# A decoder layer on one core: low parts of the first weights on GpSimd, convolution taps all on VectorE, and the compression's layout and banks moved

## The chip, the cores and the metric

The kernel runs on one core of a Trainium2 chip. The metric is device time in microseconds (us), as the median over runs. Engines are called as the profile calls them: PE (TensorE, matmuls), PEld (its weight loads), DVE (VectorE), ACT (ScalarE), POOL (GpSimd) and SP (SyncE, which here issues most DMAs). SBUF is the on-chip memory, PSUM the banks that PE writes its sums to. Each engine works through its own list of instructions strictly in order; semaphores hold an instruction until its inputs are there.

## The reference

One layer of a hybrid decoder with 256 positions and width 1024, all in float32:

```python
h = rms_norm(x, norm_mix_g)
x = x + hybrid_mixer(h, ...)        # convolution module and sparse attention, gated, one projection
x = x + cross_attention(rms_norm(x, norm_x_g), mem, xq_w, xkv_w, xo_w)
x = x + swiglu(rms_norm(x, norm_ffn_g), ffn_in_w, ffn_out_w)
return rms_norm(x, final_norm_g)
```

The change concerns the mixer. It multiplies `h` by one wide matrix whose column blocks are `u` (2048 columns for the convolution), `q` (16 heads of 64), `kc, vc, ks, vs, kw, vw` (four groups of 64 each), the logits of the heads' gates, and `g_conv, g_attn`. What it does with them:

```python
a, gt = split(u); v = a * sigmoid(gt)
v = causal_depthwise_conv(v, width=31) + bias         # 1024 channels, 31 taps each
conv_out = silu(layer_norm(v)) @ conv_pw_w
# compression: 15 blocks of 32 positions, step 16, for kc and vc
z = blocks + pos; k_cmp, v_cmp = silu(einsum("nlgd,lde->nge", z, w1)) @ w2
s_c = q @ k_cmp * scale + bias; p_cmp = softmax(s_c, masked)
# two more softmax branches, over selected blocks and over a window
o = g0 * o_cmp + g1 * o_selected + g2 * o_window
y = sigmoid(g_conv) * conv_out + sigmoid(g_attn) * o
```

With 256 positions all four blocks of 64 are selected and the window of 512 covers everything, so the two branches have the same scores and differ in their values only.

## The kernel before

**Products.** A float32 product is made of three fast matmuls: each operand is split into a high part and the rest. For a half chunk of weights (128 partitions x 1024) ACT copies the raw half to the high part (L174, names ending in `h`), and DVE subtracts that from the raw half (L175, names ending in `l`). PE then runs three groups of eight matmuls: high weights with high data, high weights with low data, low weights with high data. A chunk of 256 columns has two halves. Chunks are used in the order u0 to u7 (convolution), kc, vc, q0 to q3, ks, kw, vs, vw, ga0 to ga3 (`g_attn`), gc0 to gc3 (`g_conv`), then the values and keys of the cross attention and so on, up to the FFN (`f`, `fo`).

**Buffers.** The raw halves of all chunks take turns in four SBUF buffers (tag `w`, 512 KB each), the high parts in five (`whi`) and the low parts in five (`wlo`). SP issues the transfer of a raw half as soon as its buffer is free, that is when ACT's copy and the subtraction of the half four places earlier are done. So the low part of one half decides when the half four places later can start to load.

**Order.** A scheduler of the tile framework simulates the program when it is built, and writes each engine's list in the order of that simulation. A lower priority number goes first; `behind(marks)` makes an instruction come after given ones. `in_line()` keeps matmuls in program order. `convolve(...)` emits taps of the convolution with a priority 1500 later than the place where they stand: they fill time that the engine has left in the simulation.

**Convolution.** Channels come in eight blocks of 128 (`vt`), each with 31 taps over 256 positions. Before, two generators share them. `taps_v` runs 108 taps and their starts on DVE, with accumulators in two PSUM banks (tag `pt`). `taps_g` lets ACT multiply (L419, 104 products of 128x256) and POOL add pairs of blocks in SBUF (L421, 61 sums of 128x512), with every sixth product on POOL (L417). `joined` adds the parts. `yt` holds the result, `ysum` its sum over blocks for the layer norm.

**Compression.** `kvt` holds kc and vc by position. `hidden()` makes `z_ps`, 32 matmuls whose moving operand takes every 16th position, and from it `zz`. `compressed()` multiplies `zz` by the second layer, into `kc_ps` (bank `s0`) and `vc_ps` (bank `o`). `nsc` holds the scores of the compressed branch, first their bias (from `cb_ps`, L469), to which DVE adds `cs_ps` (L676).

**Attention.** Heads go in eight pairs. For a pair PE writes scores `s` (L712, L714), DVE evicts them with the bias `nb` and takes the extremes (L717, L722), ACT takes the exponentials (L732, L736), DVE scales (L744, L746), PE transposes into `pt_a`, `pt_b` (L757), ACT copies them to `ptt_a`, `ptt_b` (L760), and PE multiplies by the values into `o` (L767 to L775). For the compressed branch DVE and ACT normalise `nsc` (L814 to L826), PE transposes it into `pc_ps` (L858), ACT copies it to `pct` (L860); `vals` (L839) holds the values. The gc chunks are multiplied in between the first pairs.

**End.** Of the FFN's last part, sums of `fo` weights called `tr` (L1084) are made on DVE in `side` for a product of seven blocks with fewer multiplications; the first four of them stand early, around 483 us.

Of the kernel before, what the change touches and what calls it, by code (L numbers as in the profile page):

```python
# [97 lines left out]
def tile_hybrid_block(  # L98
# [71 lines left out]
    def split(w, shape, name):  # L170
        hi = small(f"{name}h", shape, F32R, tag="whi", bufs=5)
        lo = small(f"{name}l", shape, F32R, tag="wlo", bufs=5)
        with behind(*first.get(name, ())):
            copy = nc.scalar.activation(hi, w, AF.Copy)  # L174
            splits[name] = copy, nc.vector.tensor_tensor(out=lo, in0=w, in1=f(hi[:]), op=ALU.subtract)  # L175
# [215 lines left out]

    yt = long("yt", 6)

    def taps_v(j, ts, out):

        acc = [aux(f"yp{j + i}", [P, S], "pt", 2) for i in range(2)]
        for t in ts:
            for i in range(2):
                k = j + i
                v, w = vt[k][:, t:t + S], col(PP_DW + TAPS * k, t)  # L400
                if t == ts[0]:
                    nc.vector.tensor_scalar(out=acc[i], in0=v, scalar1=w, scalar2=col(PP_DB, k) if t == 0 else 0.0,
                                            op0=ALU.mult, op1=ALU.add)
                else:
                    nc.vector.scalar_tensor_tensor(out=out[:, i] if t == ts[-1] else acc[i], in0=v, scalar=w,  # L405
                                                   in1=acc[i], op0=ALU.mult, op1=ALU.add)
                yield

    def taps_g(j, ts):

        y = yt[:, j:j + 2]
        for t in ts:
            pr = y if t == 0 else small(f"vw{j}_{t}", [P, 2, S], tag="vw", bufs=4)
            for i in range(2):
                v, w = vt[j + i][:, t:t + S], col(PP_DW + TAPS * (j + i), t)
                if t % MIX == MIX - 1:
                    nc.gpsimd.tensor_scalar(out=pr[:, i], in0=v, scalar1=w, scalar2=0.0, op0=ALU.mult, op1=ALU.add)  # L417
                else:
                    nc.scalar.activation(pr[:, i], v, AF.Identity, scale=w, bias=col(PP_DB, j + i) if t == 0 else 0.0)  # L419
            if t > 0:  # L420
                nc.gpsimd.tensor_tensor(out=y, in0=y, in1=pr, op=ALU.add)  # L421
            yield

    def joined(j, other):
        nc.gpsimd.tensor_tensor(out=yt[:, j:j + 2], in0=yt[:, j:j + 2], in1=other, op=ALU.add)
        yield


    part01, part67 = (small(n, [P, 2, S], tag="pr", bufs=4) for n in ("part01", "part67"))
    taps = range(TAPS)  # L430
    on_v = chain(taps_v(0, taps[FIRST_G:], part01), taps_v(2, taps, yt[:, 2:4]), taps_v(6, taps[LAST_G:], part67))
    on_g = chain(taps_g(0, taps[:FIRST_G]), joined(0, part01), taps_g(6, taps[:LAST_G]), taps_g(4, taps), joined(6, part67))

    def convolve(n_v, n_g, *marks):

        here = tc.cur_priority
        tc.cur_priority = here + 1500
        with behind(*marks):
            for _ in range(n_v):
                next(on_v, None)  # L440
            for _ in range(n_g):
                next(on_g, None)
# [21 lines left out]
    nsc = small("nsc", [P, 2, HEADS, 16])  # L464
    cb_ps = aux("cb_ps", [P, 2, 16, HEADS], "s", 2)
    for qb in range(2):
        for i, ns in enumerate(CGROUPS):
# [1 line left out]
            nc.tensor.matmul(cb_ps[:, qb, n0:n1].rearrange("p n h -> p (n h)"), lhsT=cbt[:, i, qb * P:qb * P + P],  # L469
                             rhs=relt[:, RT_CB + 16 * n0:RT_CB + 16 * n1], start=True, stop=True)  # L470
# [19 lines left out]
    zz = small("zz", [P, 2, 4 * 64], tag="pr", bufs=4)  # L490
    nc.vector.memset(zz, 0.0)
    kvt = [long(f"{n}t", slot, (P, GROUPS + 1, S)) for n, slot in (("k", 11), ("v", 13))]
    for kv, name in enumerate(("kc", "vc")):
# [2 lines left out]
        nc.scalar.activation(kc[0:64, 0:GROUPS:2, :], ps[0:64], AF.Copy)
        nc.scalar.activation(kc[64:128, 0:GROUPS:2, 0:S - 1], ps[0:64, :, 1:S], AF.Copy)
        nc.scalar.activation(kc[0:64, 1:GROUPS:2, :], ps[64:128], AF.Copy)
        act = nc.scalar.activation(kc[64:128, 1:GROUPS:2, 0:S - 1], ps[64:128, :, 1:S], AF.Copy)
        nc.vector.memset(kc[:, GROUPS], 0.0)  # L500
        vec = nc.vector.tensor_copy(kc[:, GROUPS, 0:32:2], ppt[:, PP_POS + 16 * kv:PP_POS + 16 * kv + 16])
        convolve(10 - 2 * kv, 5, act, vec)
# [6 lines left out]
    def hidden():  # L509
# [3 lines left out]
        for l in range(16):  # L513
            for kv in range(2):
                nc.tensor.matmul(z_ps[HD * kv:HD * kv + HD], lhsT=w1t[:, kv, l], rhs=kvt[kv][:, :, 2 * l:2 * l + 16 * (NCMP - 1) + 1:16],
                                 start=l == 0, stop=l == 15)
# [13 lines left out]
    def compressed():  # L530

        kc_ps = aux("kc_ps", [P, GROUPS, 16], "s0", 1)
        nc.tensor.matmul(kc_ps, lhsT=ppt[:, PP_W2K:PP_W2K + P], rhs=zz[:, 0, :64].rearrange("p (g n) -> p g n", g=GROUPS),
# [880 lines left out]
```

## Time and profile before

| | us |
|---|---|
| median of 3 runs | 558.39 (558.24 to 559.12) |
| profiled execution | 558.58 |
| its span | 556.7 |
| PE busy in the span | 544.6 |
| DVE busy | 469.2 |
| ACT busy | 387.6 |
| POOL busy | 147.7, most of it between 46 and 179 us |

The span is that of the engines' instructions; 1.9 us of the execution lie around it. In rows of a timeline the first number is the start from the span's beginning, the second the duration, `x8` a run of eight like instructions, and a bracket gives the idle time ahead of the row and what ended it. The ends of matmuls are modelled and overlap, so starts are compared with starts. The granted clock of PE is 1.00 over the whole span.

### The profile page before, as it was taken

What the parts mean: (1) busy time and instruction counts of PE and PEld (TensorE: products, weight loads), DVE (VectorE), ACT (ScalarE), POOL (GpSimd) and SP (SyncE); (2) the same over time, 40 slices, a digit from 0 to 9 for tenths busy, and PEclk for the clock granted to TensorE, in tenths of its full rate; (3) what the DMA queues carried; (4) which work ended last, traced back from release to release, by engine and by line L of the source; (5) the groups of instructions that cost most, each with busy time, mean ns of one, the idle gap of its engine ahead of it and who ended that gap; (6) DMA issues with size and microseconds to landing.
All of it is one profiled execution on the core that took longest, in us unless ns stands there. A gap on an engine that the chain in (4) does not pass through costs nothing. (4 is left out here: it accounts for less than half of the span.)

```text
span 556.7 us, 10584 instructions
## 1 busy us (share of the span) xinstructions
PE 544.6 (98%) x3976; PEld 505.3 (91%) x3976; DVE 469.2 (84%) x874; ACT 387.6 (70%) x724; POOL 147.7 (27%) x121
## 2 busy tenths in 40 slices
PE   9999999989999999999999999999999999999995
PEld 8999999989999998998999999988888888788884
DVE  3889998999989998895768676577899998799896
ACT  4678769999777897779646655466666676566653
POOL 0006999999998000300003100150000000000000
PEclk9999999999999999999999999999999999999999
DMA  8949725434563554335555733444646664454632
GB/s 303 400 137 323 281 92 160 155 104 166 156 225 106 170 195 131 98 109 170 189 180 177 273 118 98 172 146 159 218 153 192 200 203 161 152 174 167 195 108 75
DMA packets 29154, 97.31 MB, mean 175 GB/s; under 512 B 3120, under 2 KB 5680, under 8 KB 28848
## 3 DMA queue, kind: packets, MB, share of 16 engines
q1 hardware_dynamic: 28384, 95.42, 51.4%
q10 hardware_dynamic: 720, 1.23, 0.6%
q8 instruction: 31, 0.51, 0.4%
q14 instruction: 19, 0.16, 0.1%
HBM read 95.39 MB, written 1.25 MB: 174 GB/s over the span
## 5 line engine op out<-in xcount | busy, mean ns | idle before, releaser
L421 POOL TENSOR_TENSOR yt<-yt,vw 128x512 f32<-128x512 f32 x61 | 102.0, 1673 | 49.8 <-DVE yp L405 46.2
L419 ACT ACTIVATE vw<-vt,ppt 128x256 f32<-128x256 f32 x104 | 45.4, 498 | 8.6 <-POOL yt L421 8.3
L1140 PE MATMUL ps_f<-g,f_0h 128*128 128x512 f32 x176 | 48.4, 397 | 1.2 <-DVE ab L1144 1.2
L1140 PE MATMUL ps_f<-g,f_1h 128*128 128x512 f32 x176 | 48.9, 397 | 0.0
L405 DVE SCALAR_TENSOR_TENSOR yp<-vt,ppt,yp 128x256 f32<-128x256 f32 x108 | 45.4, 477 | 0.2
L1140 PEld LDWEIGHTS ps_f<-g,f_1h 128*128 128x128 f32 x176 | 32.8, 188 | 7.5
L1140 PEld LDWEIGHTS ps_f<-g,f_0h 128*128 128x128 f32 x176 | 30.0, 188 | 5.4 <-DVE ab L1144 1.4
L175 DVE TENSOR_TENSOR f_1l<-f,f_1h 128x1024 fp32r<-128x1024 f32 x22 | 27.5, 1248 | 4.4 <-ACT f_1h L174 2.6
L1142 PEld LDWEIGHTS ps_f<-g,f_0l 128*128 128x128 f32 x176 | 27.0, 189 | 3.9
L174 ACT ACTIVATE f_1h<-f 128x1024 fp32r<-128x1024 f32 x22 | 23.3, 1057 | 7.3 <-PE ps_xo L239 3.7
L175 DVE TENSOR_TENSOR f_0l<-f,f_0h 128x1024 fp32r<-128x1024 f32 x22 | 26.8, 1218 | 1.7 <-ACT f_0h L174 1.7
L1142 PE MATMUL ps_f<-g,f_0l 128*128 128x256 f32 x176 | 28.2, 282 | 0.0
L1142 PE MATMUL ps_f<-g,f_1l 128*128 128x256 f32 x176 | 26.5, 281 | 0.0
L174 ACT ACTIVATE f_0h<-f 128x1024 fp32r<-128x1024 f32 x22 | 23.1, 1051 | 1.3 <-PE ps_xo L239 1.3
L732 ACT ACTIVATE p<-p,mins 128x256 f32<-128x256 f32 x32 | 15.9, 502 | 10.7 <-DVE mins L717 10.7
L1142 PEld LDWEIGHTS ps_f<-g,f_1l 128*128 128x128 f32 x176 | 23.3, 188 | 0.0
L1143 ACT ACTIVATE ab<-ps_f 128x256 f32<-128x256 f32 x44 | 16.5, 376 | 8.8 <-PE ps_f L1142 8.1
L1144 DVE TENSOR_TENSOR ab<-ps_f,ab 128x256 f32<-128x256 f32 x44 | 18.3, 419 | 4.5 <-ACT ab L1143 4.2
L283 ACT ACTIVATE uh<-sl 128x256 fp32r<-128x256 f32 x22 | 9.1, 415 | 15.8 <-DVE sl L1148 15.8
L1147 ACT ACTIVATE sl<-ab 128x256 f32<-128x256 f32 x22 | 9.2, 417 | 13.6 <-DVE ab L1145 13.5
L923 POOL COPY acc<-s_wo 128x256 f32<-128x256 f32 x1 | 0.7, 658 | 63.6 <-ACT s_wo L916 63.6
L417 POOL TENSOR_SCALAR vw<-vt,ppt 128x256 f32<-128x256 f32 x18 | 16.1, 905 | 0.5
(621 smaller groups left out, 1682.9 us busy)
## 6 DMA issues: line engine op xcount, KB each, us to landing
f<-in_wst_dram SPq DMA_DIRECT2D x44, 512.0 KB, 5.4
fo<-in_wfo_dram SPq DMA_DIRECT2D x22, 512.0 KB, 3.7
u<-in_wst_dram SPq DMA_DIRECT2D x14, 512.0 KB, 6.2
q<-in_wst_dram SPq DMA_DIRECT2D x8, 512.0 KB, 5.4
ga<-in_wst_dram SPq DMA_DIRECT2D x8, 512.0 KB, 4.4
gc<-in_wst_dram SPq DMA_DIRECT2D x8, 512.0 KB, 4.6
v<-in_wst_dram SPq DMA_DIRECT2D x8, 512.0 KB, 6.5
pw<-in_wst_dram SPq DMA_DIRECT2D x8, 512.0 KB, 4.3
```

The source lines that it names most:

```text
L174: copy = nc.scalar.activation(hi, w, AF.Copy)
L175: splits[name] = copy, nc.vector.tensor_tensor(out=lo, in0=w, in1=f(hi[:]), op=ALU.subtract)
L405: nc.vector.scalar_tensor_tensor(out=out[:, i] if t == ts[-1] else acc[i], in0=v, scalar=w, in1=acc[i], op0=ALU.mult, op1=ALU.add)
L417: nc.gpsimd.tensor_scalar(out=pr[:, i], in0=v, scalar1=w, scalar2=0.0, op0=ALU.mult, op1=ALU.add)
L419: nc.scalar.activation(pr[:, i], v, AF.Identity, scale=w, bias=col(PP_DB, j + i) if t == 0 else 0.0)
L421: nc.gpsimd.tensor_tensor(out=y, in0=y, in1=pr, op=ALU.add)
L732: exp.append(nc.scalar.activation(p1[k][:, br], p1[k][:, br], AF.Exp, scale=-1.0, bias=mins[:, hd, 1, br:br + 1], accum_out=sums[:, hd, 1, ...
L1140: nc.tensor.matmul(ps, lhsT=hs[kb // 4][0][:, kb % 4, cs], rhs=fg[:, :, kb], start=kb == 0, stop=False)
L1142: nc.tensor.matmul(ps[:, 1], lhsT=hs[kb // 4][1][:, kb % 4, cs], rhs=fg[:, 0, kb], start=False, stop=kb == NB - 1)
L1143: nc.scalar.activation(ab[:, b], ps[:, 0], AF.Copy)
L1144: nc.vector.tensor_tensor(out=ab[:, b], in0=ps[:, 1], in1=ab[:, b], op=ALU.add)
L1147: silu = nc.scalar.activation(sl, ab[:, 0], AF.Silu)
```

## The change

It has five parts.

1. `split` makes the low parts of u1 to ga1 on GpSimd (POOL) in place of DVE: 38 halves (`aside`).
2. All 248 taps run on DVE, block pair by block pair, with accumulators in the two PSUM banks `pt`. ACT's products and POOL's sums and joins are gone. POOL keeps `ysum`.
3. `kvt` is laid out by place within a block of 16, so that the moving operand of `z_ps` is contiguous. `hidden()` follows q1 as a whole (`in_line`). `compressed()` puts both products into one bank `o` and follows vs.
4. Banks: `rel_ps` goes to `s0`, `cb_ps` to `o` and into line ahead of kc, the second `cs_ps` to `o`, `gt_ps` to `s0`. Copies of q go by 64x512 in place of 64x256. The low parts of ga2_1 and ga3_1 are told to come after the sums into `nsc`.
5. The first `tr` sums at the end stand behind the marks of the last FFN part.

```diff
@@ split @@
+            eng = nc.gpsimd if name[:-2] in aside else nc.vector
-            splits[name] = copy, nc.vector.tensor_tensor(out=lo, in0=w, in1=f(hi[:]), op=ALU.subtract)
+            splits[name] = copy, eng.tensor_tensor(out=lo, in0=w, in1=f(hi[:]), op=ALU.subtract)
+    aside = CHUNKS[CHUNK_AT["u1"]:CHUNK_AT["ga2"]]
@@ convolution @@
+    def tapped(j):
         acc = [aux(f"yp{j + i}", [P, S], "pt", 2) for i in range(2)]
+        for t in range(TAPS):
             for i in range(2):
                 k = j + i
                 v, w = vt[k][:, t:t + S], col(PP_DW + TAPS * k, t)
+                if t == 0:
+                    nc.vector.tensor_scalar(out=acc[i], in0=v, scalar1=w, scalar2=col(PP_DB, k), op0=ALU.mult, op1=ALU.add)
                 else:
+                    nc.vector.scalar_tensor_tensor(out=yt[:, k] if t == TAPS - 1 else acc[i], in0=v, scalar=w, in1=acc[i],
+                                                   op0=ALU.mult, op1=ALU.add)
                 yield
-    def taps_g(j, ts):
...
+    taps = chain(*[tapped(j) for j in range(0, NB, 2)])
-        convolve((0, 4, 6, 6, 8, 8, 10, 12)[j], (0, 2, 3, 3, 4, 4, 4, 4)[j], act, vec)
+        convolve(13 * (j > 0), act, vec)
@@ tables @@
-    rel_ps = aux("rel_ps", [P, 384], "s", 2)
+    rel_ps = aux("rel_ps", [P, 384], "s0", 1)
-    cb_ps = aux("cb_ps", [P, 2, 16, HEADS], "s", 2)
+    cb_ps = aux("cb_ps", [P, 2, 16, HEADS], "o", 1)
...
+    last[:] = [mm]
@@ compression @@
-    kvt = [long(f"{n}t", slot, (P, GROUPS + 1, S)) for n, slot in (("k", 11), ("v", 13))]
+    kvt = [long(f"{n}t", slot, (P, 8, GROUPS + 1, 16)) for n, slot in (("k", 11), ("v", 13))]
...
-                nc.tensor.matmul(z_ps[HD * kv:HD * kv + HD], lhsT=w1t[:, kv, l], rhs=kvt[kv][:, :, 2 * l:2 * l + 16 * (NCMP - 1) + 1:16],
-                                 start=l == 0, stop=l == 15)
+        with in_line():
+                    mm = nc.tensor.matmul(z_ps[HD * kv:HD * kv + HD], lhsT=w1t[:, kv, l],
+                                          rhs=kvt[kv][:, l % 8, :, l // 8:l // 8 + NCMP], start=l == 0, stop=l == 15)
...
-        kc_ps = aux("kc_ps", [P, GROUPS, 16], "s0", 1)
-        vc_ps = aux("vc_ps", [P, 2, HD], "o", 1)
+        c_ps = aux("c_ps", [P, 3, HD], "o", 1)
...
-        with behind(*last):
-            if j == 0:
-                hidden()
-            elif j == 2:
-                compressed()
+        if j == 1:
+            hidden()
...
-        convolve(2 * TAPS * br, 3 + TAPS * br, act, splits[name + "_1"][1])
+        convolve(13 + NB * TAPS * br, act, splits[name + "_1"][0])
+        if not br:
+            compressed()
@@ scores of the compressed branch, gates @@
-            cs_ps = aux(f"cs_ps{qb}", [P, HEADS, 2, 16], ("s", "pt")[qb], 2)
+            cs_ps = aux(f"cs_ps{qb}", [P, HEADS, 2, 16], *(("s", 2), ("o", 1))[qb])
...
+            first[("ga2_1", "ga3_1")[qb]] = added,
-    gt_ps = aux("gt_ps", [P, 2, ng], "o", 1)
+    gt_ps = aux("gt_ps", [P, 2, ng], "s0", 1)
@@ end @@
-        for n in range(4):
-            side(tr, w, n)
+        with behind(*marks if i == SEVEN[1] else ()):
+            for n in range(4):
+                side(tr, w, n)
```

How the lists of the engines move is seen at three places. In these rows a line number is that of the kernel they are from (the change's lines are some 2 to 21 lower), and a number behind a name tells apart buffers of one name in program order.

First PE, around the compression's second layer. Before, in the middle of q3 and ks:

```order
L239 MATMUL ps_q_1586<-hl,q_1h 128x256 x3
L533 MATMUL kc_ps<-zz,ppt 128x64
L239 MATMUL ps_q_1586<-hl,q_1h 128x256 x5
L239 MATMUL ps_q_1586<-hh,q_1l 128x256 x8
L239 MATMUL ps_ks<-hh,ks_0h 128x256 x8
L239 MATMUL ps_ks<-hl,ks_0h 128x256 x2
L538 MATMUL vc_ps<-ppt,zz 128x64 x2
L239 MATMUL ps_ks<-hl,ks_0h 128x256 x6
```

With the change, between vs and vw:

```order
L239 MATMUL ps_vs<-vs_1h,hl 128x256 x8
L239 MATMUL ps_vs<-vs_1l,hh 128x256 x8
L514 MATMUL c_ps<-zz,ppt 128x64
L517 MATMUL c_ps<-ppt,zz 128x64 x2
L239 MATMUL ps_vw<-vw_0h,hh 128x256 x8
```

Both products of `zz` stand three chunks later and together.

Second DVE, where the scores of the compressed branch are summed and their softmax begins. Before:

```order
L676 TENSOR_TENSOR nsc<-cs_ps_2152,nsc 128x256 x2
L814 TENSOR_REDUCE mc<-nsc 128x32
L815 TENSOR_TENSOR nsc<-nsc,mc 128x512
L739 SCALAR_TENSOR_TENSOR sums<-sums,igd 128x8
L175 TENSOR_TENSOR gc_1l<-gc_1_2432,gc_1h 128x1024
```

With the change:

```order
L654 TENSOR_TENSOR nsc<-cs_ps_2011,nsc 128x256
L174 TENSOR_TENSOR ga_1l<-ga_1_2201,ga_1h 128x1024
L174 TENSOR_TENSOR gc_0l<-gc_0_2261,gc_0h 128x1024
L174 TENSOR_TENSOR gc_1l<-gc_1_2291,gc_1h 128x1024
L407 SCALAR_TENSOR_TENSOR yp_1718<-vt_354,ppt,yp_1718 128x256
L407 SCALAR_TENSOR_TENSOR yp_1717<-vt_354,ppt,yp_1717 128x256
L793 TENSOR_REDUCE mc<-nsc 128x32
```

Taps of the last pair of blocks (`yp_1717`, `yp_1718`) stand between the steps, and three splits ahead of `mc`. Further on, eight more taps stand between the reduction `sumc` and the last product into `nsc`; behind that product the order is as before: eight evictions of the second head pair, `vals`, and the split of gc1's first half.

Third ACT, where the first head pair's transposed weights are copied. Before:

```order
L174 ACTIVATE gc_1h<-gc_1_2730 128x1024
L860 ACTIVATE pct<-pc_ps 128x512
L760 ACTIVATE ptt_a_2465<-pt_a_2460 128x512
L760 ACTIVATE ptt_a_2472<-pt_a_2467 128x512
L760 ACTIVATE ptt_b_2479<-pt_b_2474 128x512
L732 ACTIVATE p_2_2384,sums<-p_2_2384,mins 128x256 x2
```

With the change:

```order
L172 ACTIVATE gc_0h<-gc_0_2505 128x1024
L799 ACTIVATE nsc<-nsc 128x512
L625 ACTIVATE sga<-ps_ga_2170 128x512
L172 ACTIVATE gc_1h<-gc_1_2589 128x1024
L839 ACTIVATE pct<-pc_ps 128x512
L172 ACTIVATE gc_0h<-gc_0_2660 128x1024
L739 ACTIVATE ptt_a_2324<-pt_a_2319 128x512
L739 ACTIVATE ptt_a_2331<-pt_a_2326 128x512
L739 ACTIVATE ptt_b_2338<-pt_b_2333 128x512
L711 ACTIVATE p_2_2243,sums<-p_2_2243,mins 128x256 x2
```

The copy of gc3's first half (`gc_0_2660`) now stands ahead of the three copies; before, it stood behind them and behind the exponentials of the second pair. The copy of gc2's first half (`gc_0_2505`) now stands ahead of the exponential of `nsc`; before, it stood behind it.

More of the change, by code (lines that the diff above doesn't have):

```diff
@@ L31 @@
 NCMP = 15
-MIX = 6
-FIRST_G, LAST_G = 23, 10
 WARM = 10
@@ L400, in taps_v, with convolve @@
                 v, w = vt[k][:, t:t + S], col(PP_DW + TAPS * k, t)
-                if t == ts[0]:
-                    nc.vector.tensor_scalar(out=acc[i], in0=v, scalar1=w, scalar2=col(PP_DB, k) if t == 0 else 0.0,
-                                            op0=ALU.mult, op1=ALU.add)
-                else:
-                    nc.vector.scalar_tensor_tensor(out=out[:, i] if t == ts[-1] else acc[i], in0=v, scalar=w,
-                                                   in1=acc[i], op0=ALU.mult, op1=ALU.add)
+                if t == 0:
+                    nc.vector.tensor_scalar(out=acc[i], in0=v, scalar1=w, scalar2=col(PP_DB, k), op0=ALU.mult, op1=ALU.add)
+                else:
+                    nc.vector.scalar_tensor_tensor(out=yt[:, k] if t == TAPS - 1 else acc[i], in0=v, scalar=w, in1=acc[i],
+                                                   op0=ALU.mult, op1=ALU.add)
                 yield
-    def taps_g(j, ts):
[L411 to L434, printed above, removed]
+    taps = chain(*[tapped(j) for j in range(0, NB, 2)])
+    def convolve(n, *marks):
         here = tc.cur_priority
@@ L438, in convolve @@
         with behind(*marks):
[L439 to L442, printed above, removed]
+            for _ in range(n):
+                next(taps, None)
         tc.cur_priority = here
@@ L495, in tile_hybrid_block @@
         kc = kvt[kv]
[L496 to L502, printed above, removed]
+        for g in range(2):
+            for odd in range(2):
+                at = ps[HD * g:HD * g + HD].rearrange("p b (m l o) -> p b l m o", l=8, o=2)[:, :, :, :, odd]
+                act = nc.scalar.activation(kc[HD * odd:HD * odd + HD, :, g:GROUPS:2].rearrange("p l b m -> p b l m"), at, AF.Copy)
+        nc.vector.memset(kc[:, :, GROUPS], 0.0)
+        vec = nc.vector.tensor_copy(kc[:, :, GROUPS, 0:2],
+                                    ppt[:, PP_POS + 16 * kv:PP_POS + 16 * kv + 16].rearrange("p (m l) -> p l m", m=2))
+        convolve(14, act, vec)
     kcp = small("kcp", [P, GROUPS, 2, 16], F32R)
@@ L530, in compressed @@
     def compressed():
-        kc_ps = aux("kc_ps", [P, GROUPS, 16], "s0", 1)
-        nc.tensor.matmul(kc_ps, lhsT=ppt[:, PP_W2K:PP_W2K + P], rhs=zz[:, 0, :64].rearrange("p (g n) -> p g n", g=GROUPS),
-                         start=True, stop=True)
-        part(kcp[:, :, 0], kcp[:, :, 1], kc_ps[:])
-        vc_ps = aux("vc_ps", [P, 2, HD], "o", 1)
-        for i in range(2):
-            nc.tensor.matmul(vc_ps[:, i], lhsT=zz[:, 1, i * P:i * P + P], rhs=ppt[:, PP_W2V:PP_W2V + HD],
-                             start=True, stop=True)
+        c_ps = aux("c_ps", [P, 3, HD], "o", 1)
+        kc_ps, vc_ps = c_ps[:, 0].rearrange("p (g n) -> p g n", g=GROUPS), c_ps[:, 1:3]
+        with in_line():
+            nc.tensor.matmul(kc_ps, lhsT=ppt[:, PP_W2K:PP_W2K + P], rhs=zz[:, 0, :64].rearrange("p (g n) -> p g n", g=GROUPS),
+                             start=True, stop=True)
+            for i in range(2):
+                mm = nc.tensor.matmul(vc_ps[:, i], lhsT=zz[:, 1, i * P:i * P + P], rhs=ppt[:, PP_W2V:PP_W2V + HD],
+                                      start=True, stop=True)
+        last[:] = [mm]
+        part(kcp[:, :, 0], kcp[:, :, 1], kc_ps)
         nc.scalar.activation(vcs, vc_ps, AF.Copy)
@@ L675, in compressed_scores @@
             for i in range(2):
-                nc.vector.tensor_tensor(out=nsc[:, qb], in0=cs_ps[:, :, i], in1=nsc[:, qb], op=ALU.add)
+                added = nc.vector.tensor_tensor(out=nsc[:, qb], in0=cs_ps[:, :, i], in1=nsc[:, qb], op=ALU.add)
+            first[("ga2_1", "ga3_1")[qb]] = added,
     few = compressed_scores()
```

37 lines of the change are left out of this document (17 added, 20 removed).

## The prediction

> **What bounds the kernel now.** I read the page's table of engines first, then the waits of PE, then PE's timeline at each of those waits.
>
> ```profile
> PE 544.6 (98%) x3976; PEld 505.3 (91%) x3976; DVE 469.2 (84%) x874; ACT 387.6 (70%) x724; POOL 147.7 (27%) x121
> 82.44 2.02 PE L469 MATMUL cb_ps<-tables 128*128 128x48 f32 x16 [0.85 <-DVE vt L449]
> 118.96 0.43 PE L533 MATMUL kc_ps<-zz,ppt 128*128 128x64 f32 x2 [1.11 <-DVE zz L525]
> 123.44 0.63 PE L538 MATMUL vc_ps<-ppt,zz 128*128 128x64 f32 x4 [1.28 <-DVE zz L527]
> 164.62 0.47 PE L712 MATMUL s<-kdh,qt 128*128 128x512 f32 x1 [0.40 <-DVE nsc L676]
> 485.40 1.20 PE L1140 MATMUL ps_f<-g,f_0h 128*128 128x512 f32 x4 [1.22 <-DVE ab L1144]
> ```
>
> PE is busy 98% of the span. Work taken off another engine therefore buys only what PE waits for, and behind PE's start these five rows are all that it waits for: 0.85 + 1.11 + 1.28 + 0.40 + 1.22 = 4.86 us. Every other microsecond that DVE, ACT or POOL saves is worth nothing, while a new wait of PE costs its full length.
>
> **What the change removes.** The four stalls up to 165 us have causes that the diff takes away. cb_ps moves from a bank of the scores in the middle of kc to the place right behind u7, in a bank of its own. The two products of the compression's second layer stood inside q3 and ks, right behind a DVE result; they now follow vs, two to three chunks of weights later. The cs_ps tiles no longer hold the bank that s_1 needs. At 485 us DVE stood in front of a tr sum whose fo half had not landed; that sum is now held behind the last FFN part. I count all five as gone: -3.64 us up to 165 and -1.22 behind. If one stays, its own row is its price.
>
> **The compression's keys** are written by place so that z_ps reads them contiguously.
>
> ```profile
> 99.69 0.31 PE L515 MATMUL z_ps<-vt,w1t 128*64 128x75 f32 x1
> 99.82 0.31 PE L515 MATMUL z_ps<-vt,w1t 128*64 128x75 f32 x1
> 187.22 0.44 PE L772 MATMUL o<-ptt_b,vals 128*64 128x128 f32 x4
> 187.49 0.60 PE L775 MATMUL o<-ptt_a,vals 128*64 128x256 f32 x4
> ```
>
> A strided pair starts every 0.13 us, 0.065 a record; four records of the same height with a contiguous operand take 0.27, 0.068 each. So I put the layout at 0. Were half of the 32 pairs' time to go it would be -2.1, at worst strided writes by ACT cost a few tenths off PE's path.
>
> **Low parts on POOL.** 38 halves of 128x1024 leave DVE. Before shows POOL only at 128x512 and 128x256.
>
> ```profile
> 166.48 1.29 POOL L421 TENSOR_TENSOR yt<-yt,vw 128x512 f32<-128x512 f32 x1
> 50.74 10.76 POOL L421 TENSOR_TENSOR yt<-yt,vw 128x512 f32<-128x512 f32 x6
> 297.24 0.80 POOL L925 TENSOR_TENSOR acc<-acc,s_wo 128x256 f32<-128x256 f32 x1
> 119.88 1.11 PE L239 MATMUL ps_q<-hh,q_1l 128*128 128x256 f32 x8
> 120.83 1.11 PE L239 MATMUL ps_ks<-hh,ks_0h 128*128 128x256 f32 x8
> ```
>
> From 0.80 to 1.29 is 1.9 ns an element, so 1024 take 1.29 + 512 x 1.9 = 2.27 us when POOL runs freely. The upper bound is twice the disturbed 10.76/6 = 1.79, 3.6 us. PE uses one half in three groups of 0.95, 2.85 us. I take 2.5: the disturbed sums ran beside DVE splits with two operands in SBUF, and those splits leave while the taps that stay read one operand from PSUM. So POOL keeps up: 0, with a cover of 0.35 us a half. With 3.2 it would fall 38 x 0.35 = 13 us behind, less the 3 us that five buffers give.
>
> **The taps** all go to DVE, 248 instead of 108 on it. ACT's 45 us of products disappear, and with them nothing that PE waits for. Five taps stand between 157.30 and 159.26 below: 0.39 each. 140 x 0.39 = 55 us come, 38 x 1.14 = 43 us of splits go (1.14 from 185.32 to 186.46). DVE gets some 11 us more up to 190 us. Its order carries the last 25 taps into the stage of scores and softmax, in between the steps of nsc. That is where I see the loss.
>
> ```profile
> 157.30 2.04 DVE L405 SCALAR_TENSOR_TENSOR yp<-vt,ppt,yp 128x256 f32<-128x256 f32 x5
> 159.26 0.86 DVE L405 SCALAR_TENSOR_TENSOR part<-vt,ppt,yp 128x256 f32<-128x256 f32 x2
> 162.09 0.47 PE L712 MATMUL s<-kdh,qt 128*128 128x512 f32 x1
> 170.06 0.41 DVE L717 CUSTOM_DVE_ANT_0 p<-s,nb 128x256 f32<-128x256 f32 x1
> 172.28 0.87 DVE L676 TENSOR_TENSOR nsc<-cs_ps,nsc 128x256 f32<-128x256 f32 x2
> 175.76 0.63 ACT L820 ACTIVATE nsc<-nsc 128x512 f32<-128x512 f32 x1 [0.67 <-DVE nsc L815]
> 176.30 1.05 ACT L174 ACTIVATE gc_0h<-gc 128x1024 fp32r<-128x1024 f32 x1
> 178.07 0.62 DVE L821 TENSOR_REDUCE sumc<-nsc 128x32 f32<-128x512 f32 x1
> 178.06 0.33 SPq L203 DMA_DIRECT2D gc<-in_wst_dram  x1
> 181.75 1.06 ACT L174 ACTIVATE gc_1h<-gc 128x1024 fp32r<-128x1024 f32 x1 [1.54 <-DMA gc<-in_wst_dram]
> 181.90 0.42 DVE L717 CUSTOM_DVE_ANT_0 p<-s,nb 128x256 f32<-128x256 f32 x1
> 182.72 0.60 PE L858 MATMUL pc_ps<-cpt,nsc 128*128 128x128 f32 x4
> 184.12 1.29 DVE L839 TENSOR_TENSOR vals<-vcs,cpt 128x512 f32<-128x512 f32 x2
> 184.21 1.08 ACT L760 ACTIVATE ptt_a<-pt_a 128x512 f32<-128x512 f32 x2
> 185.32 1.22 DVE L175 TENSOR_TENSOR gc_0l<-gc,gc_0h 128x1024 fp32r<-128x1024 f32 x1
> 185.64 0.53 ACT L732 ACTIVATE p<-p,mins 128x256 f32<-128x256 f32 x1
> 186.46 1.22 DVE L175 TENSOR_TENSOR gc_1l<-gc,gc_1h 128x1024 fp32r<-128x1024 f32 x1
> 186.57 1.47 SPq L203 DMA_DIRECT2D gc<-in_wst_dram  x2
> 190.69 1.06 ACT L174 ACTIVATE gc_0h<-gc 128x1024 fp32r<-128x1024 f32 x1 [0.94 <-DMA gc<-in_wst_dram]
> 191.65 0.49 ACT L732 ACTIVATE p<-p,mins 128x256 f32<-128x256 f32 x1
> ```
>
> **The new wait.** Raw halves share four buffers, so the first half of gc3 takes the buffer of gc1's first half, and its transfer starts when DVE has made that half's low part: split from 185.32, issued at 186.57, ACT copies it at 190.69, 4.1 us after the issue (the half issued at 178.06 took 3.7; I use 4.0). Before, this copy stands behind the ptt copies and the exponentials, and costs only ACT 0.94. The changed order puts it ahead of the three ptt copies, for which PE's o waits. On DVE the split is still behind the last nsc product, eight evictions and vals, and that row is now later for the taps.
>
> Step by step. PE fills the first scores at 162.09 - 3.24 = 158.85, so DVE's evictions begin near 159.5 (at 158.9 if nothing delays them, near 160.2 if the queue of taps is full). Then 2.22 for eight evictions, four taps 1.56, two sums 0.9, ga3's and gc0's splits 2 x 1.14: 166.5. That split frees the buffer of gc2's first half, whose copy now stands ahead of nsc's exponential on ACT: 4.0 to its start, 0.96, and 0.54 for the exponential, 172.0. From the reduction to the end of the last product before takes 181.90 - 178.07 = 3.83, now with eight taps, 3.12, in between: 178.95. That is the time at which PE reaches pc_ps (182.72 - 3.64 = 179.08), so nothing is lost yet. Evictions 2.22, vals 1.20, gc1's split 1.14: 183.5. Transfer 4.0, copy 0.96, three ptt copies 185.64 - 184.21 = 1.43 and 0.3 to the start on PE: 190.2. PE would be there at 187.22 - 3.64 = 183.6: a stall of 6.6 us, which leaves PE 3.0 us later than before. Both gaps that I chose can shift this by about 1 us either way.
>
> One head pair later the scaling on DVE waits for exponentials that now start behind the late ptt copies: 0 to 0.9 us, I take 0.5.
>
> **PE after a long idle.** No stall of before is longer than 1.28 us, so what 6.6 us do to the clock is not in it. Its start gives one bound.
>
> ```profile
> 1.05 4.63 PE L337 MATMUL warm<-ones 128*128 128x128 f32 x20 [1.05 <-DVE eps_t L157]
> 5.48 7.42 PE L269 MATMUL ps_k<-mem_t,k0w 128*128 128x256 f32 x32
> ```
>
> The first 20 records start every 4.43/20 = 0.22 us for 128 columns; the next take 0.23 for 256 columns of the same type. So PE ran at half pace for 4.4 us and lost 2.2, although the granted clock reads 1.00. After the stall the loss lies between 0 (the 1.28 us rows) and 2.2; I take the middle, 1.1, as 6.6 us is far from both. The Trainium skill, TensorE: Matmul & The Clock Gate, Part 1, says that an idle window of about 3.4 us drops the array to half rate and that it takes some 3.4 us of work to return. By that rule the term is an estimated 1.7 and the sum 0.6 higher; the start's rows agree in kind, with 4.4 us.
>
> **Sum**, against the profiled execution's 558.58 us (span 556.7): +3.0 - 1.22 + 0.5 + 1.1 = +3.4, 562.0. The median of the runs is 0.19 lower, so 561.8.
>
> **Rivals.** *No hold-up* (0.20, faster): gc3's half is there in time, or the evictions come early enough that PE hardly waits. Speaking for it: the chain has nine steps, each sized from a different place. Against: the buffer's release at 185.32 and the issue at 186.57 are in the trace, and only the order on ACT has to be as written. It would leave -4.86 and about 1 us of DVE's lateness at the next head pair: 554.5. *Half a hold-up* (0.12, no change): the chain 3 us shorter, a stall under 3.6 us without the clock's loss: 3.4 - 3.0 - 1.1 = -0.7, about 558. *POOL too slow* (0.10, slower): it decides from 2.85 + 3/38 = 2.93 us a half. At 3.2 it adds 10 us that PE waits for in u to ga, and the hold-up shrinks since DVE is then less behind: 565 to 570. For it: 1.79 disturbed. Against: what disturbed it leaves.
>
> **How the numbers follow.** My forecast, slower through the hold-up on ACT, has 0.58, with its own range 559.6 to 564.6 from the bounds above. What can be told from no change is 0.2%, 1.1 us. Slower has 0.58 + 0.10 = 0.68, same 0.12, faster 0.20. The range from 554.6 to 565.5 leaves out about half of the faster rival and most of the one with POOL, under 2 in 10.
>
> **What would show it.** Right: a wait of PE o on ACT ptt_b of 5 to 8 us near 183 to 191, ACT idle before gc_0h on a transfer, POOL's 128x1024 at 2.2 to 2.8 us, none of the five rows above. Wrong: no such wait, waits of PE on POOL low parts between 45 and 145 us, or the five stalls replaced by others of DVE.

## The result, and the profile after

The changed kernel takes 564.86 us (median of 4 runs, 564.24 to 565.86); the kernel before, beside it, 558.75. The ratio is 1.0106, with a 95% interval of 1.0088 to 1.0125: 1.1% slower. The forecast was 561.8 and slower. The profiled execution has a span of 563.0 us, 6.3 more than before. Executions of any kernel that ran over 1.5% longer than its fastest one, at a lower granted clock, are left out of all times below.

The engines' line of the page, then the list of PE's waits (in total, how many, the longest), both of the changed kernel:

```profile
PE 543.6 (97%) x3976; PEld 504.5 (90%) x3976; DVE 464.7 (83%) x956; ACT 343.7 (61%) x606; POOL 117.7 (21%) x78
```

```profile
PE pt_a L736 <- DVE yt L407: 8.5, 1, 8.5
PE pc_ps L837 <- DVE nsc L805: 2.5, 1, 2.5
```

Left out is the row of PE's start, 1.1 us before and after. All five waits of before are gone. In their place stand two, both on DVE, and the longer one is not the one that was forecast: PE waits at the first head pair's transposes for `yt`, the last taps of the convolution. PE's timeline there:

```profile
177.53 0.66 PE L837 MATMUL pc_ps<-cpt,nsc 128*128 128x128 f32 x4 [2.46 <-DVE nsc L805]
186.67 1.97 PE L736 MATMUL pt_a<-cpt,p 128*128 128x128 f32 x8 [8.48 <-DVE yt L407]
192.65 0.59 PE L746 MATMUL o<-pct,vals 128*128 128x256 f32 x2
```

What PE waits for is on DVE (timeline of the same stage):

```profile
170.84 0.69 DVE L800 TENSOR_REDUCE sumc<-nsc 128x32 f32<-128x512 f32 x1 [2.07 <-ACT nsc L799]
...
176.79 0.68 DVE L805 TENSOR_TENSOR nsc<-nsc,sumc 128x512 f32<-128x512 f32 x1
179.61 1.28 DVE L818 TENSOR_TENSOR vals<-vcs,cpt 128x512 f32<-128x512 f32 x2
180.82 1.22 DVE L174 TENSOR_TENSOR gc_0l<-gc,gc_0h 128x1024 fp32r<-128x1024 f32 x1
...
184.23 1.21 DVE L174 TENSOR_TENSOR gc_1l<-gc,gc_1h 128x1024 fp32r<-128x1024 f32 x1
185.36 0.87 DVE L407 SCALAR_TENSOR_TENSOR yp<-vt,ppt,yp 128x256 f32<-128x256 f32 x2
186.14 0.86 DVE L407 SCALAR_TENSOR_TENSOR yt<-vt,ppt,yp 128x256 f32<-128x256 f32 x2
```

The taps accumulate in two PSUM banks of the tag `pt`, and the two `pt_a` of a head pair take turns in the same two. The last four taps stand behind `vals` and four splits, so the first bank comes free at 186.6 and the second at 187.0, while PE was ready at 178.19.

DVE is not busy all the way there. At 168.77 it stops for 2.07 us until ACT's exponential of `nsc` is done. ACT has that exponential behind its copy of gc2's first half, and the copy waits for a transfer:

```profile
169.23 1.06 ACT L172 ACTIVATE gc_0h<-gc 128x1024 fp32r<-128x1024 f32 x1 [1.90 <-DMA gc<-in_wst_dram]
```

DVE works without a break from there to the last tap. So, as an estimate from these rows, about 2 of the 2.46 us at pc_ps, and about 2 us of the lateness of the taps, come from ACT's order at this copy. No run changes this copy alone.

PE's start at the same records, changed kernel minus before, gives the balance (us; negative is ahead):

| place (start before) | difference | what happened since the row above |
|---|---|---|
| third group of ks (124.68) | -7.39 | cb, kc and vc stalls gone, `z_ps` faster |
| gc0 (178.9) | -7.82 | products of `zz` moved here, s stall gone |
| pc_ps (182.72) | -5.19 | wait of 2.46 |
| pt_a (183.16) | +3.51 | wait of 8.48 |
| o (186.69) | +5.96 | PE at half pace |
| FFN sums (475.82) | +5.89 | nothing |
| after the tr sums (488.31) | +4.40 | ps_f stall gone |
| last product (547.70) | +5.43 | waits below what the list shows |
| end of the span | +6.3 | DVE's last rows |

The half pace is in the granted clock. These are stretches of 4 us with the busy time of PE, its weight loads, DVE, ACT and POOL (in brackets the number of instructions); the next column is the clock (1.00 in the stretch ahead of these), the last two are DMA:

```profile
178.00:182.00 4.00, 0.18 (x2) 0.00 (x0) 4.00 (x18) 0.60 (x1) 0.00 (x0) 0.61 0.11 32
182.00:186.00 4.00, 0.00 (x0) 0.00 (x0) 4.00 (x6) 0.00 (x0) 0.00 (x0) 0.50 0.75 227
186.00:190.00 4.00, 3.33 (x16) 3.33 (x17) 1.01 (x3) 2.73 (x4) 2.76 (x3) 0.50 0.71 236
190.00:194.00 4.00, 4.00 (x28) 3.52 (x29) 1.53 (x3) 4.00 (x18) 0.52 (x1) 0.68 0.31 110
```

From pt_a to o PE took 5.98 us, and 3.53 before: 2.45 lost.

The forecast hold-up stands in the same trace. The changed kernel's ACT:

```profile
186.10 1.06 ACT L172 ACTIVATE gc_0h<-gc 128x1024 fp32r<-128x1024 f32 x1 [7.29 <-DMA gc<-in_wst_dram]
187.82 0.60 ACT L739 ACTIVATE ptt_a<-pt_a 128x512 f32<-128x512 f32 x1 [0.66 <-PE pt_a L736]
```

and SP's queue, with the transfer that this copy waits for, issued behind DVE's split from 180.82:

```profile
182.10 1.48 SPq L203 DMA_DIRECT2D gc<-in_wst_dram  x2
```

ACT is idle for 7.29 us on the transfer, 4.0 us from issue to copy. But the copy ends at 187.16, and ACT gets the first pt_a only at 187.82. So the two limits lie less than a microsecond apart, and the trace alone does not say what would be left if one were gone.

The last two views answer the steps on POOL (groups, mean ns) and on `z_ps` (PE's timeline):

```profile
L174 POOL TENSOR_TENSOR u_1l<-u,u_1h 128x1024 fp32r<-128x1024 f32 x7 | 18.2, 2603 | 0.0
L174 POOL TENSOR_TENSOR q_0l<-q,q_0h 128x1024 fp32r<-128x1024 f32 x4 | 9.7, 2433 | 1.2 <-ACT q_0h L172 1.2
```

```profile
101.81 0.23 PE L493 MATMUL z_ps<-kt,w1t 128*64 128x75 f32 x1
101.88 0.23 PE L493 MATMUL z_ps<-kt,w1t 128*64 128x75 f32 x1
```

A low part takes POOL 2.4 to 2.6 us, and PE never waits for one. A pair of `z_ps` records starts every 0.065 us; before, every 0.13.

### The profile page after: what moved, and what is told of

It reads as the page before. It is cut to its first block, busy times and chain, and to the rows that moved or that the text cites. A ratio compares the mean times of both kernels' runs of the same rounds, so it can differ in the third digit from the quotient of the medians.

```text
span 563.0 us, 10472 instructions
## 1 busy us (share of the span) xinstructions
PE 543.6 (97%) x3976; PEld 504.5 (90%) x3976; DVE 464.7 (83%) x956; ACT 343.7 (61%) x606; POOL 117.7 (21%) x78
## 4 chain that ended last, share of the span: by engine, by line
PE 83%; DVE 9%; DMA 5%; ACT 1%; issue 1%; ACTq 0%; DVEq 0%; SPq 0%
PE ps_f L1120 15%; PE ps_u L239 8%; PE ps_f L1122 7%; PE ps_pw L239 4%; PE ps_q L239 4%; PE ps_xq L239 4%; PE ps_wo L239 4%; PE ps_v L239 4%; PE ps_xo L239 4%; PE ps_gc L239 3%; PE ps_k L239 3%; PE ps_ga L239 3%; DMA fo<-in_wfo_dram 3%; DVE fo_1l L174 2%; DVE tr L1063 2%; PE pt_a L736 1%
## 5 line engine op out<-in xcount | busy, mean ns | idle before, releaser
L407 DVE SCALAR_TENSOR_TENSOR yp<-vt,ppt,yp 128x256 f32<-128x256 f32 x232 | 93.7, 480 | 0.3
L174 POOL TENSOR_TENSOR u_0l<-u,u_0h 128x1024 fp32r<-128x1024 f32 x7 | 17.6, 2512 | 32.1 <-DVE kt L476 30.3
L174 POOL TENSOR_TENSOR u_1l<-u,u_1h 128x1024 fp32r<-128x1024 f32 x7 | 18.2, 2603 | 0.0
L736 PE MATMUL pt_a<-cpt,p 128*128 128x128 f32 x64 | 9.3, 292 | 8.5 <-DVE yt L407 8.5
L172 ACT ACTIVATE fo_1h<-fo 128x1024 fp32r<-128x1024 f32 x10 | 10.6, 1056 | 8.9 <-DMA fo<-in_wfo_dram 5.5
```

The costliest lines, as they stand in the source:

```text
L174: splits[name] = copy, eng.tensor_tensor(out=lo, in0=w, in1=f(hi[:]), op=ALU.subtract)
L407: nc.vector.scalar_tensor_tensor(out=yt[:, k] if t == TAPS - 1 else acc[i], in0=v, scalar=w, in1=acc[i], op0=ALU.mult, op1=ALU.add)
L736: mm = nc.tensor.transpose(ps[:, i], src, ident)
```

## The experiments

Three explanations were open. *The copy on ACT*: the forecast, gc3's first half ahead of the ptt copies. *The shared bank*: pt_a cannot start before the last tap has left it. *Too much work on DVE*: neither place is the cause, DVE has more to do between 140 and 190 us than time, and whatever comes last in its order makes PE wait.

### The copy on ACT put behind the ptt copies

```diff
         if hp == 0:
+            first["gc3_0"] = copies[-1],
```

> The change, with one edit: gc3's first half is copied by ACT behind the first pair's three ptt copies; banks and everything else as changed. Theory A (the hold-up is ACT's copy of gc3's half standing ahead of the ptt copies): the stall of 8.5 us goes, and the 2.4 us of slow PE behind it; about 554. Theory B (the transposes wait for the two PSUM banks that the last pair's taps hold until 187 us): the wait of pt_a on DVE yt stays at 8 to 8.5 us; 564 to 565.

Measured: 564.06 us (562.98 to 565.70), ratio to before 1.0089 (1.0056 to 1.0122), not to be told from the change. PE's longest wait:

```profile
PE pt_a L736 <- DVE yt L407: 8.0, 1, 8.0
```

The place of this copy is not what binds in the changed kernel. The copy of gc2's first half stays ahead of the exponential of `nsc` here, and DVE waits 2.01 us for it as before.

### The last taps without the shared banks

The last pair of blocks accumulates in `yt` itself, in SBUF.

```diff
-        acc = [aux(f"yp{j + i}", [P, S], "pt", 2) for i in range(2)]
+        acc = [yt[:, j + i] if j == 6 else aux(f"yp{j + i}", [P, S], "pt", 2) for i in range(2)]
```

> The change, with one edit: the taps of the last pair of blocks accumulate in SBUF (in yt itself) and not in the two PSUM banks. The order that the scheduler then writes also puts gc3's copy on ACT behind the ptt copies, so neither hold is left. Both theories: no wait of pt_a on yt, PE not over 3 us idle there, no slow stretch of PE; 564.9 - 8.5 - 2.4 = about 554. If a third thing holds the transposes, the time stays over 558.

Measured: 563.55 us (561.80 to 569.82, three executions), ratio 1.0105 (1.003 to 1.018); about 554 was expected. The profiled execution took 561.8. The scheduler also moved gc3's copy behind the ptt copies, so this run has neither hold. PE's waits:

```profile
PE pt_a L736 <- DVE p L725: 2.7, 1, 2.7
PE s L691 <- DVE nsc L654: 2.6, 1, 2.6
PE pc_ps L837 <- DVE nsc L805: 1.6, 1, 1.6
PE pt_b L736 <- DVE mins L701: 0.8, 1, 0.8
```

The wait for `yt` is gone, so the bank was what held pt_a. But it is not what the time was lost by alone: four waits for other rows of DVE take its place, 7.7 us in place of 11.0, and the time is not to be told from that of the change. At `o` PE is 1.36 us ahead of the kernel before, and behind the gc chunks, at `mu`, 3.07 late.

### The same, with gc3's copy forced ahead of the ptt copies

For this the splits of gc1, gc2 and gc3's first half are also written earlier in the program, with a later priority; the lines below show only the order on ACT.

```diff
+        if hp == 0:
...
+            hold.append(splits["gc3_0"][0])
...
-        copies.append(nc.scalar.activation(t, ps, AF.Copy))
+        with behind(*hold):
+            copies.append(nc.scalar.activation(t, ps, AF.Copy))
```

> As the run with the free banks, but gc3's copy is put ahead of the ptt copies on ACT as in the change. Theory A as a limit of its own: PE does its transposes early and then waits at o for ptt_b until about 189 us (186.1 + 1.06 + 1.4 + 0.3 in the changed kernel's times), a stall of 5 to 8 us; 559 to 563. Theory B alone: no such stall, about 554.

Measured: 565.72 us (565.01 to 566.78), ratio 1.0118 (1.0082 to 1.0154). PE's timeline:

```profile
192.23 0.69 PE L752 MATMUL o<-ptt_b,vals 128*64 128x128 f32 x4 [5.93 <-ACT ptt_b L740]
```

This is the forecast wait, of the forecast size (6.6 forecast, 5.93 measured). Ahead of it PE is 0.99 us ahead of the kernel before, behind it 5.01 late: 6.0 us. So the mechanism exists and costs nearly what was worked out, where pt_a does not hold PE ahead of it. In the changed kernel it does. The time is above the 559 to 563 that were expected: PE also waits 2.7 us at `s`, 1.7 at pc_ps and 0.8 at pt_b, much as in the run before.

### Parts 3 and 4 alone

The kernel before, with the layout, the moved products and the banks; taps, low parts and the tr sums as before.

```diff
-            eng = nc.gpsimd if name[:-2] in aside else nc.vector
+            eng = nc.vector
...
-    taps = chain(*[tapped(j) for j in range(0, NB, 2)])
+    on_v = chain(taps_v(0, taps[FIRST_G:], part01), taps_v(2, taps, yt[:, 2:4]), taps_v(6, taps[LAST_G:], part67))
+    on_g = chain(taps_g(0, taps[:FIRST_G]), joined(0, part01), taps_g(6, taps[:LAST_G]), taps_g(4, taps), joined(6, part67))
```

> The kernel before with only the compression's layout and place, the banks, the merged copies of q and the held splits of ga2 and ga3 (parts 3 and 4); low parts and taps as before, tr sums as before. If the 7.8 us that PE is ahead by at gc in the changed kernel come from these parts: 558.5 - 7 to 8 = 550.5 to 552. If parts 1 and 2 are needed for it (DVE too late without them): 553 to 558.

Measured: 564.45 us (561.65 to 565.83), ratio 1.0090 (1.0063 to 1.0118). PE is 7.1 us ahead at ks, 2.8 at ga, 4.9 late at gc. It waits 4.8 us for the gates' sigmoid on ACT, 2.3 for ACT's and DVE's parts of kw, 1.3 for `nsc`. The time is above both expectations. Up to ks the gain is nearly that of the changed kernel (7.39), so it comes from these parts. But with ACT still multiplying taps, other rows of ACT and DVE are late next, and the gain is lost before the head pairs. That keeping it takes less work on ACT and DVE is what this suggests; it was not separated from their order.

### All low parts on DVE

```diff
-            eng = nc.gpsimd if name[:-2] in aside else nc.vector
+            eng = nc.vector
```

> The change with all low parts back on DVE, the taps on DVE as changed. From vt's first block at 24 us of DVE's work to the first sums into nsc the changed order holds 99 us of DVE work in about 118 us; 38 splits add 43. Theory C: DVE is 25 us short, PE waits for low parts and the time is 580 to 600. If DVE had room that the order wastes: under 570.

Measured: 595.55 us (595.31 to 595.79), ratio 1.0662 (1.0636 to 1.0687). PE has one wait of length:

```profile
PE pt_a L736 <- DVE yt L407: 41.1, 1, 41.1
```

38 splits of 1.14 are 43 us of work for DVE; the wait at the bank grows by 32.6 us. PE waits for no low part: DVE puts taps off, and three quarters of the debt are paid at the one place where PE needs the banks back. The time is in the range expected if DVE is short of time, but the waits for low parts that were expected with it did not come.

### More low parts on POOL

The list `aside` goes on to the chunk `v0`. Beside ga2, ga3 and gc it so holds pw, wo and xq, which stand between gc and v.

```diff
-    aside = CHUNKS[CHUNK_AT["u1"]:CHUNK_AT["ga2"]]
+    aside = CHUNKS[CHUNK_AT["u1"]:CHUNK_AT["v0"]]
```

> The change, with the low parts of ga2, ga3 and gc0 to gc3 on GpSimd too: 12 more halves, 13.7 us less on DVE between 139 and 190 us, where GpSimd had nothing to do from 139 on. Theory C (DVE has more work in this stage than PE leaves it time for; which queue or bank shows the wait is secondary): waits of PE at pc_ps and pt_a fall from 11 us to under 3, no slow stretch of PE; 564.9 - 8 - 2.4 - 2 = 551 to 554. If order or banks alone are the cause and DVE's amount of work is not: the wait moves by less than 4 us, over 558. If GpSimd is too slow for it: new waits of PE on ga and gc low parts.

Measured: 569.72 us (569.70 to 570.97), ratio 1.0207 (1.0185 to 1.0228). At `mu` PE is only 0.09 us late, 5.8 better than the changed kernel; then it loses 11.2 from wo and xq through the cross attention. Before that, too, there is a new cost: PE waits 4.3 us at pc_ps. DVE's timeline there, and POOL's:

```profile
164.71 2.40 DVE L794 TENSOR_TENSOR nsc<-nsc,mc 128x512 f32<-128x512 f32 x1
168.36 0.67 DVE L800 TENSOR_REDUCE sumc<-nsc 128x32 f32<-128x512 f32 x1
169.35 2.04 DVE L723 TENSOR_SCALAR p<-p,sums 128x256 f32<-128x256 f32 x1
171.31 2.44 DVE L725 TENSOR_SCALAR p<-p,sums 128x128 f32<-128x128 f32 x1
```

```profile
164.13 2.43 POOL L174 TENSOR_TENSOR gc_0l<-gc,gc_0h 128x1024 fp32r<-128x1024 f32 x1
168.81 2.43 POOL L174 TENSOR_TENSOR gc_1l<-gc,gc_1h 128x1024 fp32r<-128x1024 f32 x1 [2.24 <-ACT gc_1h L172]
171.19 2.48 POOL L174 TENSOR_TENSOR gc_0l<-gc,gc_0h 128x1024 fp32r<-128x1024 f32 x1
```

A scaling row of DVE that takes 0.28 us alone takes 2.44 here; both long ones end 0.1 to 0.2 us behind POOL's split (171.39 and 171.24, 173.75 and 173.67). The Trainium skill, SBUF — State Buffer, Who interferes with whom, says that the two engines share a pair of ports and that whichever issues first keeps it for its whole instruction; the trace agrees, for DVE's subtraction with two operands in SBUF and for its scaling in SBUF. The reduction `mc` at 163.34 kept its 0.67 within POOL's split from 161.75 to 164.18, and the taps ahead of it, whose accumulator is in PSUM, start every 0.39 beside POOL as without it.

### Part 5 undone

```diff
-        with behind(*marks if i == SEVEN[1] else ()):
-            for n in range(4):
-                side(tr, w, n)
+        for n in range(4):
+            side(tr, w, n)
```

> The change with part 5 undone: the first tr sums at the end stand where they stood before. In the changed kernel PE gained 1.5 us at ps_f and lost 1.0 before the last matmul and 0.9 behind it. If these belong together: the stall of 1.2 to 1.5 at ps_f returns, the 1.9 go, and the time is 0.3 to 0.5 us lower, 564.4. If the late losses have another cause: 566.

Two executions took 563.27 and 563.33 us; there is no interval. A stall of 0.8 us at ps_f is back, but PE's lateness stays flat at 4.88 us from there to the last product, where the changed kernel goes from 4.40 to 5.43 and loses 0.87 more on DVE behind it. The span is 1.4 us shorter, but 0.6 of that is there at the FFN sums already, ahead of the edited place. In this pair part 5 so removes its stall and gives 0.8 us more back at the end; two later kernels that differ in it, and in ACT's copy, have medians 0.2 us apart. Its size is not settled.

### Both of the last two

> Both edits of the two runs before this one: the low parts of ga2 to gc3 on GpSimd too, and the first tr sums early. Theory C: 551 to 553.5, 0.3 to 0.5 below the run with the more on GpSimd alone. Order or banks alone: over 558.

Measured: 567.81 us (566.24 to 571.53), ratio 1.0175 (1.0135 to 1.0215). PE is 0.9 us ahead at `mu` and 10.3 late behind the cross attention: the loss from wo on is again 11.2 us. The last kernel below, with all of gc but none of pw, wo and xq on POOL, doesn't have it: 0.85 ahead at `mu`, 1.3 at the end. So it comes with these three chunks.

### Four low parts more on POOL

POOL is idle from 140 to 160 us in the changed kernel, and free of softmax rows on DVE beside it. Here ga2 and ga3 go to POOL, and gc stays on DVE.

```diff
-    aside = CHUNKS[CHUNK_AT["u1"]:CHUNK_AT["ga2"]]
+    aside = CHUNKS[CHUNK_AT["u1"]:CHUNK_AT["gc0"]]
```

> The changed kernel with one more piece of work moved: the low parts of ga2 and ga3 are also made on GpSimd, those of gc stay on VectorE. DVE has 4 x 1.14 = 4.6 us less in 139 to 160 us, and GpSimd is through with its low parts by about 150 us, before the softmax steps begin on DVE. If DVE's amount of work is what makes the shared bank late (the last tap then stands ahead of the norm of nsc in DVE's order), PE's wait at pt_a falls from 8.5 us to under 2, no slow stretch of PE follows (2.5 us), and the time is 553 to 557. What is left in that case is a wait of o on ACT's copies of up to 5.9 us, since the copy of gc3's first half still stands ahead of the ptt copies: then 557 to 560. If it isn't the amount but the bank's place in the order, the wait stays above 6 us and the time at 563 to 565.

Measured: 553.72 us (552.88 to 555.50), ratio 0.9911 (0.9894 to 0.9927). Four splits, 4.6 us of DVE, turn 1.1% slower into 0.9% faster. PE's timeline at the banks:

```profile
175.09 1.04 PE L736 MATMUL pt_a<-cpt,p 128*128 128x128 f32 x8
187.82 1.81 PE L736 MATMUL pt_a<-cpt,p 128*128 128x128 f32 x8 [2.03 <-DVE p L725]
```

and DVE's:

```profile
170.96 0.78 DVE L407 SCALAR_TENSOR_TENSOR yt<-vt,ppt,yp 128x256 f32<-128x256 f32 x2
171.87 1.79 DVE L805 TENSOR_TENSOR nsc<-nsc,sumc 128x512 f32<-128x512 f32 x1
186.08 1.23 DVE L174 TENSOR_TENSOR gc_1l<-gc,gc_1h 128x1024 fp32r<-128x1024 f32 x1 [0.61 <-ACT gc_1h L172]
187.22 0.35 DVE L723 TENSOR_SCALAR p<-p,sums 128x256 f32<-128x256 f32 x1
```

and ACT's, at the copy of gc3's first half:

```profile
176.74 0.62 ACT L739 ACTIVATE ptt_b<-pt_b 128x512 f32<-128x512 f32 x1
182.28 1.06 ACT L172 ACTIVATE gc_0h<-gc 128x1024 fp32r<-128x1024 f32 x1 [0.96 <-DMA gc<-in_wst_dram]
```

The last tap now stands ahead of the norm of `nsc`, and both waits at the first head pair are gone. The copy on ACT, left as it was in the program, doesn't bind: in the order that the scheduler makes of this kernel it stands behind the ptt copies, so this run takes both holds away. The exponential of `nsc`, too, now stands ahead of the copy of gc2's first half, and DVE no longer stops for it. What is left is a wait of 2.03 us one pair later: DVE scales `p` behind two splits, of which the second waits for ACT. And the low clock follows it, which cost 1.5 us more (last section).

The time is within what was expected if the amount of work is the cause. But the amount went with the order: 4.6 us less work brought the last tap 15.3 us forward, from 187.0 to 171.7. Of these, 2.1 are DVE's stop for the exponential, and 8.6 are the norm, eight evictions, `vals` and four splits, which stood ahead of the last four taps and now stand behind them. The `nsc` norm took 1.79 us here in place of 0.68, beside POOL's `ysum`, which the earlier taps let start at that moment. A kernel with the same work and only the last four taps moved ahead was not run, so how much the order alone is worth stays open.

### With the copy on ACT and the tr sums as in the first and the seventh experiment

> As the run before it, and beside that the copy of gc3's first half behind the ptt copies on ACT, and the first tr sums at their old place. If the first hold is the bank (through DVE's work) and the second is ACT's order, both are gone here: no wait of PE above 2 us between 160 and 200 us, 564.9 - 8.5 - 2.5 - 0.8 = 553, with the wait at pc_ps gone 551. If taking both leaves DVE short of time further on, as in the run that gave the last taps accumulators in SBUF, PE loses 2 to 4 us again between 187 and 210 us: 555 to 557.

Measured: 553.49 us (551.90 to 554.97), ratio 0.9902 (0.9885 to 0.9919), not to be told from the run before it. The waits at the first pair are gone and 2.0 us are left at the second, as there: the trace is that of the second expectation, the time lies between the two.

### gc0 on POOL as well

```diff
-    aside = CHUNKS[CHUNK_AT["u1"]:CHUNK_AT["gc0"]]
+    aside = CHUNKS[CHUNK_AT["u1"]:CHUNK_AT["gc1"]]
```

> As the run before it, with the low part of gc0 on GpSimd as well, 2.3 us less on DVE. GpSimd then makes a low part at the moment at which DVE takes the sums of scores and starts the softmax. If DVE's amount of work decides, equal or up to 1 us faster than the run before it. If GpSimd holds DVE up there (the scaling rows took 2.0 to 2.4 us in place of 0.3 in the run with far more on GpSimd), 1 to 3 us slower.

Measured: 550.36 us (549.76 to 550.62), ratio 0.9844 (0.9831 to 0.9857): the fastest of all, 8.6 us below the kernel before. PE's waits, all of them behind its start:

```profile
PE o L751 <- ACT ptt_b L739: 0.6, 1, 0.6
PE ps_f L1120 <- DVE ab L1124: 0.4, 1, 0.4
```

Up to 1 us faster was expected; it was 3.1. `p` of the second pair is scaled at 184.19 (187.22 with ga2 and ga3 alone), now ahead of the two splits that it stood behind, and the wait of 2.0 goes. POOL's gc splits run at 154.56 and 161.47, where DVE has taps and evictions from PSUM; only a small scaling row (`igc`, 1.45 in place of 0.18) is held up by them. This kernel also has the edits on ACT's copy and on the tr sums; what they add was not measured apart from it.

### All of gc on POOL

```diff
-    aside = CHUNKS[CHUNK_AT["u1"]:CHUNK_AT["gc1"]]
+    aside = CHUNKS[CHUNK_AT["u1"]:CHUNK_AT["pw0"]]
```

> As the one with ga2 and ga3, with all low parts of gc0 to gc3 on GpSimd, 9.2 us less on DVE between 158 and 200 us, and eight GpSimd subtractions of 2.4 us among the softmax steps. If only the amount of DVE's work counted, it would be the fastest of the four, 550 to 552. If GpSimd's subtractions hold up DVE's scaling rows, each of the eight costs the chain of nsc up to 2 us: 558 to 564, with waits of PE at pc_ps and at the second head pair.

Measured: 557.52 us (556.97 to 558.60), ratio 0.9979 (0.9968 to 0.9990): 7.2 us slower than with gc0 alone. DVE has 6 x 1.14 = 6.8 us less to do, and PE waits at pc_ps again. Its longest wait, and the rows of DVE that grew:

```profile
PE pc_ps L837 <- DVE nsc L805: 3.2, 1, 3.2
```

```profile
164.31 2.42 DVE L794 TENSOR_TENSOR nsc<-nsc,mc 128x512 f32<-128x512 f32 x1
168.95 2.04 DVE L723 TENSOR_SCALAR p<-p,sums 128x256 f32<-128x256 f32 x1
170.92 2.45 DVE L725 TENSOR_SCALAR p<-p,sums 128x128 f32<-128x128 f32 x1
```

The three rows have grown by 5.6 us together (0.68, 0.35 and 0.28 alone). PE also waits 1.7 us at the second head pair, as expected in that case; the time is just below the 558 to 564 that went with it. In these kernels taking work off DVE helps up to the rows of the softmax, and costs from there.

## Why the prediction was right or wrong

**Direction right, size off by 3 us, binding wait not the one named.** The forecast 561.8 lies 3.1 below the 564.86 measured. That is inside the whole range, and 0.3 above the range that the hold-up on ACT was given (559.6 to 564.6).

**The new wait.** The step "PE waits at o for ptt_b, 6.6 us" described a wait that exists (5.93 when it stands alone) but is hidden behind another, 8.48 us at pt_a. What failed is an omission: the prediction followed DVE's chain to the split of gc1's first half and not to the end of the taps. It knew that 25 taps were carried into the scores, and that the accumulators were in the banks `pt`; that pt_a takes the same banks was not followed. Its chain ended 1.4 us early, at 186.10 for 187.5. The last link held, 4.0 from the issue to the copy. An earlier one did not: the split that frees gc2's buffer ended 3.0 us sooner than forecast, at 163.46, but the copy of that half came 5.8 us behind it, where 4.0 was taken.

**Evictions to pc_ps.** "Nothing is lost yet" was wrong: PE waited 2.46 us. PE was ready at 175.07, 4.0 sooner than the prediction had it (179.08), while DVE's norm ended only 1.5 sooner (177.47 for 178.95). The stop behind ACT's copy of gc2's first half is in the prediction's chain; it was counted as free because PE was thought to be later.

**Stalls removed.** -3.64 was taken up to gc0; PE was 7.82 ahead. Of the difference 2.1 is `z_ps`: the layout was put at 0, its lower bound was right (32 pairs, 0.13 to 0.065). The mistake was to compare half a pair with one record of `o`. The two records of a pair run side by side, so the pair has to be compared with one record. The Trainium skill, SBUF — State Buffer, Door 1: The DMA port swizzle, has the rule that was passed over: float32 read in steps beyond 16 bytes pays a penalty; the operand of before stepped by 64, and the trace agrees. About 1 us of the other 2.1 may be that a stall costs more from start to start than the idle time in its bracket: 0.17 to 0.27 more at pc_ps, pt_a and ps_f, which makes about 0.9 for four (an estimate). The rest stays open. The kernel with gc0 on POOL keeps these gains: its PE is 8.4 us ahead of before at the last product.

**POOL.** 2.5 was taken, 2.43 to 2.60 measured (means of groups), no wait: right. The reason fits, too: with taps in PSUM beside it POOL's groups are at most 0.2 us longer in the mean than its shortest.

**PE after a long idle.** 1.1 was taken as a middle, 2.45 measured. The granted clock shows it: 0.50 from 182 to 190 us, and the mean of 0.68 up to 194 puts the return near 192.6, some 6 us after PE's start. The rule of the Trainium skill that the prediction quotes gave an estimated 1.7, nearer; its 3.4 us of work to return were 5.9 here.

**End.** The ps_f stall went as forecast (-1.49 for -1.22). That part 5 would cost 1.9 us in small losses behind it was not foreseen.

**Sum.** -7.82 + 2.63 + 8.70 + 2.45 - 0.07 - 1.49 + 1.03 + 0.87 = +6.3, where the prediction had -3.64 + 6.64 + 1.1 + 0.5 - 1.22 = +3.4. Ahead of the head pairs 4.2 us more were gained than forecast, from pc_ps to `o` 6.0 more lost, at the next head pair 0.6 less (0.5 was put down, -0.07 measured), and at the end 1.6 more. That the total came out 3 us off is so partly luck: the steps were further off than the sum.
